# Stick-breaking attention and short convolution layer on one Trainium2 core: the last sixteen keys padded to 128 rows, Silu in one step, a first phase in written order, and a square root in the last norm

## The chip, the cores and the metric

The kernel runs on one core of one Trainium2 chip. The time is device microseconds of one execution of the whole layer, from a matrix of 256 tokens by 4096 channels to one of the same shape. The kernel before took 1779.79 us (median of three runs, 1779.18 to 1781.87). A separate execution was profiled; its own time was 1778.96 us and its profile spans 1777.2 us. Engines have the profile's names: PE does matrix products (PEld is its loading of the stationary operand), DVE and POOL do elementwise work, ACT does activation functions, copies and casts, SP issues most of the transfers between HBM and on-chip memory.

## The reference

One layer: 16 learned meta tokens are put ahead of the 256 tokens (272 positions), normed, and projected by one 4096 x 16384 matrix into eight parts of 2048 columns. Four serve attention (q, k, v and a gate), four a short convolution (B, C, h and a gate z). Each half is multiplied by the Silu of its gate, normed in groups of 128 channels, and a 4096 x 4096 matrix maps both back.

```
h = rmsnorm(x, norm_g)
p = h @ w_in
q, k, v, g_attn, b_conv, c_conv, h_conv, z_conv = jnp.split(p, cuts, axis=-1)
o = stick_breaking_attention(heads(q), heads(k), heads(v))   # 16 heads of 128
o = group_rmsnorm(o * jax.nn.silu(g_attn), attn_norm_g, ATTN_HEADS)
y = b_conv * short_conv(c_conv * h_conv, conv_w)             # 3 taps
y = group_rmsnorm(y * jax.nn.silu(z_conv), conv_norm_g, CONV_GROUPS)
hs = x + jnp.concatenate([o, y], axis=-1) @ w_out
return rmsnorm(hs, final_norm_g)[:, N_META:]
```

Attention weights are `exp(log sigmoid(z_ts) + sum of log sigmoid(-z_tj) for s < j < t)` for keys s before query t. A query block of 128 tokens sees at most 272 keys: two full blocks of 128 and 16 more.

## The kernel before, in words

**Pieces.** The weights come as a written list of pieces of 128 x 1024 numbers (`in_pieces`, and the output matrix behind it). For every piece SP loads `raw`, ACT casts it into a high part `wh` (line 409), DVE subtracts to get the low part `wl` (line 405), and PE multiplies three times, low activations by `wh`, high by `wh`, high by `wl` (lines 442 to 444 and 450 to 453), so that products of rounded parts make up a float32 product. Casts run four pieces ahead of PE (`SPLITS`), loads seven; `wh` and `wl` each have six buffers (`RING`), so ACT can cast piece i only when PE is done with piece i - 6.

**Groups.** Eight groups hold two heads and two convolution channel groups each. Pieces "A" and "B" belong to the parts q, g, B and z, which all 272 positions or 256 tokens need in full; "p" pieces make the blocks k, v, c and h of one head. From group 1 on, A and B pieces are multiplied as seven products instead of eight, with sums of tokens kept or reread (`sum`, `lent`), and two more pieces "T" and "U" are sums of A and B made by DVE (lines 426 to 431). Groups 8 to 11 are the output matrix, and eight thin pieces "o" close the list.

**Order.** A loop over pieces (`for i in range(1 - SPLITS, n)`) issues loads, PE's products and casts, and then runs tasks whose place was set by `later(piece, function)`. `plan_group` places the attention of group g: gates (`silu`), transposes of q, `scores`, `weights`, `trans`, `po` (the product of weights with values), `squares`, `norm`, `mix`. For the last group these places are counted in pieces behind its own end, `after(f, k)`. From the piece after group 0's own A and B pieces on, instructions stand on their engines in written order (`manual_schedule`, entered at `i == top[0] + 1`); ahead of that, and for the last eight pieces, a scheduler orders them. All engines take their instructions in order.

**Places that the prediction uses.** `po_mm` (line 806): five products per head. Four contract 128 keys; the fifth, line 812, contracts the last 16, with `a3` (16 x 128, weights) and `v3` (16 x 128, values). `vcopies` (line 596): ACT copies the transposed values into `vv` (16 copies of 32 x 64, line 576 in `blocks`) and `v3` (4 copies, line 605). For head 15, the last, the transpose stands at slot 13U and the copies behind slot 14U of group 7, ahead of that group's end. `silu` (line 668): ACT computes a sigmoid into a buffer, POOL multiplies it into the gate. `prep_x`: for each pair of channel blocks of x, scale by the norm's gain, cast, subtract; `finish_stats`: the rms factors of all positions, at the end of group 0. `finish(t)` (line 986): the last norm of token half t; for t = 1 it is the end of the program. It makes the reciprocal square root by nine small DVE instructions (an integer start value and two polynomial steps), then scales the 4096 columns in five parts and stores each. `WARM` products of constants stand ahead of the first piece.

Of the kernel before, what the change touches and what calls it, by code (L numbers as in the profile page):

```python
# [15 lines left out]
P = 128  # L16
D = 4096
# [20 lines left out]
WARM = 10  # L38
# [82 lines left out]
def kernel(ctx, tc, xt, xin, xm, par, fg, w1, w2, out):  # L121
# [7 lines left out]
    wk.tile([P, 46], F32, name="pad_wk")  # L129
# [16 lines left out]
    nc.vector.memset(ones, 1.0 / P)  # L146
    warm = bank("warm")
# [79 lines left out]
    rt2 = const.tile([P, 2], F32, name="rt2")  # L227
# [38 lines left out]
    def prep_x(j, parts=1):  # L266
        t = xr.pop(j)
        x = xs[j // 2][:, 2 * (j % 2):2 * (j % 2) + 2, :, :L]
        for i in range(2):
            g = pt[:, G0 + 2 * j + i:G0 + 2 * j + i + 1]  # L270
            if i or parts == 2:
                nc.vector.tensor_scalar(out=t[:, i, :], in0=t[:, i, :], scalar1=g, scalar2=None, op0=ALU.mult)
            else:
                nc.scalar.mul(out=t[:, i, :], in_=t[:, i, :], mul=g)
            if parts == 2:
                nc.scalar.copy(out=x[:, i, 0, :], in_=t[:, i, :])
                nc.vector.tensor_tensor(out=x[:, i, 1, :], in0=t[:, i, :], in1=x[:, i, 0, :].bitcast(F32), op=ALU.subtract)
        if parts == 1:
# [41 lines left out]
    def token_sums(dst, t, j):  # L320
        f = raw_sums(t, j)
        nc.scalar.copy(out=dst[:, 0], in_=f)
        nc.vector.tensor_tensor(out=dst[:, 1], in0=f, in1=dst[:, 0].bitcast(F32), op=ALU.subtract)

    mixh, mixl = [], []
# [41 lines left out]
    def split(i):  # L367
        p = pieces[i]
        if p[:2] == ("A", 0):
            prep_x(p[2], 2 if p[2] == 0 else 1)  # L370
        parts = 2 if i < 2 else 1
# [35 lines left out]
        for q in range(parts):  # L407
            c = slice(q * w // parts, (q + 1) * w // parts)
            nc.scalar.copy(out=h[:, c], in_=t[:, c])  # L409
            if parts == 2:  # L410
                low(c)
        if parts == 2:
# [33 lines left out]
    def mm_p(key, j, a, h, lo):  # L446
# [3 lines left out]
        nc.tensor.matmul(out=o, lhsT=a[1], rhs=h, start=key not in begun, stop=False)  # L450
        begun.add(key)
        nc.tensor.matmul(out=o, lhsT=a[0], rhs=h, start=False, stop=False)  # L452
        nc.tensor.matmul(out=o, lhsT=a[0], rhs=lo, start=False, stop=last)  # L453
        left[key] -= 1
# [31 lines left out]
    def mm_in(i):  # L486
# [4 lines left out]
        if p[0] == "p":  # L491
# [6 lines left out]
            return  # L498
        for q, st, c in works(i)[p[0]]:
# [3 lines left out]
            mm_p(key, p[2], st, wh[:, c], wl[:, c])  # L503
# [42 lines left out]
    def finish_stats():  # L546
# [18 lines left out]
        V.tensor_tensor(out=rt2, in0=rt, in1=rt, op=ALU.mult)  # L565
        for q in range(4):
            V.tensor_scalar(out=fac[:, 2 * q:2 * q + 2], in0=rt if q < 2 else rt2, scalar1=RS, scalar2=None,
                            op0=ALU.mult)
# [17 lines left out]
    def v_block(u, src, at_, at2):  # L586
# [4 lines left out]
        def vtrans():  # L591
            y = wk.tile([P, 416], F32, tag="zs", name=f"yv{u}")
# [3 lines left out]
        def vcopies(y):  # L596
            vv = wk.tile([P, 2 * P], F32, tag=f"vv{u % 2}", name=f"vv{u}")
            for i, k in enumerate((0, 1, 1, 1) if u < 2 else (0, 0, "p", 1) if u % 2 else (0, 0, "p", "p")):
# [3 lines left out]
            yield 1 if u < 2 else 0 if u % 2 else "p"  # L602
            v3 = wk.tile([META, P], F32, tag=f"v3{u % 2}", name=f"v3{u}")
            for i in range(4):
                A.copy(out=v3[:, 32 * i:32 * i + 32], in_=y[32 * i:32 * i + META, 2 * P:2 * P + 32])
# [24 lines left out]
    def plain_block(u, b, e):  # L630
# [17 lines left out]
    def evict(g):  # L648
# [4 lines left out]
        if g:  # L653
            p1, p5, p7, p6 = (psum.pop((g, q)) for q in (P1, P5, P7, P6))
            A.copy(out=cq[:, 0], in_=p1)
            for o, x, y, op in ((cb[:, 0], p6, cq[:, 0], ALU.add), (cq[:, 1], p7, cb[:, 0], ALU.add),
                                (cq[:, 0], d11, cq[:, 0], ALU.add), (cb[:, 1], p5, cq[:, 1], ALU.subtract),
# [10 lines left out]
    def silu(g, q):  # L668

        z = gr[g][q][1]  # L670
        s = wk.tile([P, 2, 2, P], F32, tag="u2", name=f"sg{q}{g}", bufs=2)
        for t in range(2):
            A.activation(out=s[:, t], in_=z[:, t], func=AF.Sigmoid, scale=rt[:, t:t + 1])
# [488 lines left out]
```

## Time and profile before

| | |
|---|---|
| median of three runs | 1779.79 us (1779.18 to 1781.87) |
| the profiled execution's own time | 1778.96 us |
| its span in the profile | 1777.2 us |
| around the span | 1.8 us |
| busy PE / PEld | 1762.1 / 1601.6 us |
| busy DVE / ACT / POOL | 1590.3 / 1233.1 / 151.0 us |
| moved by DMA | 410.96 MB, 231 GB/s |
| granted clock of PE over the span | 0.998 |

A timeline row reads: start, duration, engine, line, operation, written tile <- read tiles, shape, count, and in brackets how long the engine was idle ahead of it and what ended that. Products are pipelined on PE: the duration of a row is longer than the step to the next one, so rates are read from the starts. One product of two float32 operands stands as two records (x2).

### The profile page before, as it was taken

Reading aid. Unit: us, or ns where it says so; the run is one execution under the profiler, and the core shown is the slowest. Engines: PE = TensorE matmul, PEld = TensorE weight load, DVE = VectorE, ACT = ScalarE, POOL = GpSimd, SP = SyncE. Lnnn points to the kernel's source line nnn. Section 1 sums busy time; section 2 is a strip of 40 time slices with the busy share of each in tenths; the row PEclk is TensorE's granted clock in tenths of the full one; section 3 lists DMA queues with packets and bytes.
Section 4 is the critical chain, followed back from the end, with each engine's and each line's share of the span. In section 5 each row is a group of like instructions: output and inputs, shape, how many; then the busy total and the mean of one; then the engine's idle time right before and its main releaser. Section 6 shows DMA issues by size and latency. Waiting matters only on the chain.

```text
span 1777.2 us, 29833 instructions
## 1 busy us (share of the span) xinstructions
PE 1762.1 (99%) x10926; PEld 1601.6 (90%) x10926; DVE 1590.3 (89%) x1929; ACT 1233.1 (69%) x2089; POOL 151.0 (8%) x184
## 2 busy tenths in 40 slices
PE   9999999999999999999999999999999999999997
PEld 7899999999999999999999999999999988888897
DVE  6776898999999999999999999999999888989986
ACT  6755677677767776777678768776777785555553
POOL 2143110011001100010101010101010110000000
PEclk9999999999999999999999999999999999999999
DMA  8977666766676667666766676667666676676565
GB/s 316 323 238 249 226 214 216 259 214 226 218 251 219 225 226 245 215 230 222 250 215 228 213 257 215 225 218 245 213 231 226 228 236 233 231 233 213 196 224 191
DMA packets 120819, 410.96 MB, mean 231 GB/s; under 512 B 13536, under 2 KB 18784, under 8 KB 120672
## 3 DMA queue, kind: packets, MB, share of 16 engines
q1 hardware_dynamic: 116640, 405.38, 67.3%
q10 hardware_dynamic: 4032, 3.67, 0.6%
q8 instruction: 86, 1.41, 0.3%
q14 instruction: 61, 0.50, 0.1%
HBM read 395.37 MB, written 13.63 MB: 230 GB/s over the span
## 4 chain that ended last, share of the span: by engine, by line
PE 97%; DMA 1%; ACT 1%; DVE 0%; SPq 0%; issue 0%; POOL 0%; DVEq 0%; ACTq 0%
PE P L450 17%; PE P L453 17%; PE P L452 17%; PE mm L444 14%; PE mm L443 14%; PE mm L442 14%; PE mo L955 0%; PE mo L954 0%; PE mo L953 0%; PE z L755 0%; PE po L812 0%; DMA mixd<-mfh 0%; ACT wh L409 0%; DMA raw<-w 0%; PE z L754 0%; DVE wl L405 0%
## 5 line engine op out<-in xcount | busy, mean ns | idle before, releaser
L405 DVE TENSOR_TENSOR wl<-raw,wh 128x1024 fp32r<-128x1024 f32 (+3 forms) x780 | 862.2, 1135 | 77.9 <-ACT wh L409 72.2
L409 ACT CAST wh<-raw 128x1024 fp32r<-128x1024 f32 (+3 forms) x780 | 721.0, 965 | 278.0 <-PE mm L443 68.2
L442 PE MATMUL mm<-xs,wh 128*128 128x258 f32 (+1 forms) x2048 | 582.5, 284 | 0.4 <-ACT wh L409 0.4
L444 PE MATMUL mm<-xs,wl 128*128 128x258 f32 (+1 forms) x2048 | 581.7, 284 | 0.8 <-DVE wl L405 0.8
L443 PE MATMUL mm<-xs,wh 128*128 128x258 f32 (+1 forms) x2048 | 581.7, 284 | 0.0
L442 PEld LDWEIGHTS mm<-xs,wh 128*128 128x128 f32 x2048 | 385.5, 188 | 4.6 <-ACT wh L409 0.8
L443 PEld LDWEIGHTS mm<-xs,wh 128*128 128x128 f32 x2048 | 385.7, 188 | 3.7
L444 PEld LDWEIGHTS mm<-xs,wl 128*128 128x128 f32 x2048 | 385.7, 188 | 1.0 <-DVE wl L405 1.0
L409 ACT CAST wh<-t 128x1024 fp32r<-128x1024 f32 (+1 forms) x132 | 137.7, 1043 | 142.9 <-DVE t L426 123.9
L450 PE MATMUL P<-wh,xs 128*128 128x512 f32 x464 | 180.8, 390 | 1.2 <-ACT wh L409 1.2
L453 PE MATMUL P<-wl,xs 128*128 128x512 f32 x464 | 180.7, 390 | 0.2 <-DVE wl L405 0.2
L452 PE MATMUL P<-wh,xs 128*128 128x512 f32 x464 | 180.5, 389 | 0.0
L405 DVE TENSOR_TENSOR wl<-t,wh 128x1024 fp32r<-128x1024 f32 (+1 forms) x132 | 158.7, 1202 | 8.8 <-ACT wh L409 8.8
L426 DVE TENSOR_TENSOR t<-raw,raw 128x1024 f32<-128x1024 f32 (+1 forms) x132 | 164.9, 1250 | 0.0
L450 PE MATMUL P<-wh,mixl 128*128 128x512 f32 (+1 forms) x412 | 155.7, 378 | 0.0
L453 PE MATMUL P<-wl,mixh 128*128 128x512 f32 (+1 forms) x412 | 155.1, 376 | 0.0
L452 PE MATMUL P<-wh,mixh 128*128 128x512 f32 (+1 forms) x412 | 155.0, 376 | 0.0
L450 PE MATMUL P<-wh,lent 128*128 128x512 f32 x308 | 123.6, 401 | 0.0
L453 PE MATMUL P<-wl,lent 128*128 128x512 f32 x308 | 120.2, 390 | 0.0
L452 PE MATMUL P<-wh,lent 128*128 128x512 f32 x308 | 120.1, 390 | 0.0
L450 PEld LDWEIGHTS P<-wh,xs 128*128 128x128 f32 x464 | 87.1, 188 | 19.8 <-ACT wh L409 1.4
L453 PEld LDWEIGHTS P<-wl,xs 128*128 128x128 f32 x464 | 87.1, 188 | 19.3 <-DVE wl L405 1.1
(238 smaller groups left out, 2136.5 us busy)
## 6 DMA issues: line engine op xcount, KB each, us to landing
raw<-w SPq DMA_DIRECT2D x614, 512.0 KB, 4.5
lent<-sumd SPq DMA_DIRECT2D x77, 512.0 KB, 5.9
raw<-w SPq DMA_DIRECT2D x32, 384.0 KB, 3.8
sumd<-lent SPq DMA_DIRECT2D x11, 512.0 KB, 5.2
raw<-xin SPq DMA_DIRECT2D x8, 512.0 KB, 5.4
raw<-mixd SPq DMA_DIRECT2D x8, 512.0 KB, 4.6
xr<-xt SPq DMA_DIRECT2D x15, 272.0 KB, 4.9
res<-xin SPq DMA_DIRECT2D x12, 256.0 KB, 4.9
```

The lines of the kernel that those rows point to most:

```text
L405: nc.vector.tensor_tensor(out=lo[:, c], in0=t[:, c], in1=h[:, c].bitcast(F32), op=ALU.subtract)
L409: nc.scalar.copy(out=h[:, c], in_=t[:, c])
L426: nc.vector.tensor_tensor(out=s[:, :2 * hw].rearrange("p (a b) -> p a b", a=2), in0=a[:, :2 * hw].rearrange("p (a b) -> p a b", a=2), in1= ...
L442: nc.tensor.matmul(out=o, lhsT=h, rhs=x[:, 0, s:], start=k == 0, stop=False)
L443: nc.tensor.matmul(out=o, lhsT=h, rhs=x[:, 1, s:], start=False, stop=False)
L444: nc.tensor.matmul(out=o, lhsT=lo, rhs=x[:, 0, s:], start=False, stop=k == KC - 1)
L450: nc.tensor.matmul(out=o, lhsT=a[1], rhs=h, start=key not in begun, stop=False)
L452: nc.tensor.matmul(out=o, lhsT=a[0], rhs=h, start=False, stop=False)
L453: nc.tensor.matmul(out=o, lhsT=a[0], rhs=lo, start=False, stop=last)
```

## The change

1. **Padding.** `a3` and the two `v3` tiles have 128 rows instead of 16. They are zeroed once at the start, and only their first 16 rows are ever written. The product at line 812 contracts 128 rows.
2. **Silu.** ACT computes Silu into the gate itself; the sigmoid buffer and POOL's product are gone. The gate now holds the factor `rt` already, so `squares` and `fac` lose one `rt`.
3. **Written order from the first instruction.** `manual_schedule` is entered at the first turn of the loop. The first five pieces (`PARTS`) instead of two are cast in halves; the first two multiply both column halves by `wh` ahead of `wl`; the first pair of x is prepared half by half between the casts; a copy of one column (`first`) stands at the head of ACT; pairs 1 and 2 are scaled on ACT alone; sums kept for later are cast behind the B piece; `WARM` is 9.
4. **Last group.** Head 15's transpose and copies move from slots 13U and 14U to two and three pieces behind the group's end, into a `u2` buffer, one piece apart; `po`, the second `trans`, `squares` of the heads, `norm` and `mix` stand one piece later. Two of the sums in `evict` change places.
5. **Last norm.** ACT computes the square root, DVE its reciprocal and one correcting step.

```diff
-WARM = 10
+WARM = 9
+PARTS = 5
-    wk.tile([P, 46], F32, name="pad_wk")
+    wk.tile([P, 70], F32, name="pad_wk")
+    first = wk.tile([P, P], F32, tag="junk", name="first")[:, :1]
+    nc.scalar.copy(out=first, in_=ones[:, :1])
-    a3 = const.tile([META, P], F32, name="a3")
+    a3 = const.tile([P, P], F32, name="a3")
     nc.vector.memset(a3, 0.0)
+    v3s = [const.tile([P, P], F32, name=f"v3{u}") for u in range(2)]
+    for u in range(2):
+        nc.gpsimd.memset(v3s[u], 0.0)
...
         for q in range(parts):
             c = slice(q * w // parts, (q + 1) * w // parts)
+            if i == 0:
+                prep_x(0, q)
             nc.scalar.copy(out=h[:, c], in_=t[:, c])
+            if i == 0 and q == 0:
+                nc.vector.tensor_scalar(out=xr[0][:, 1, :], in0=xr[0][:, 1, :], scalar1=pt[:, G0 + 1:G0 + 2], scalar2=None, op0=ALU.mult)
             if parts == 2:
                 low(c)
+        while held and p[0] == "B":
+            held.pop()()
...
-            yield 1 if u < 2 else 0 if u % 2 else "p"
-            v3 = wk.tile([META, P], F32, tag=f"v3{u % 2}", name=f"v3{u}")
+            yield 1 if u in (0, 1, 15) else 0 if u % 2 else "p"
+            v3 = v3s[u % 2]
             for i in range(4):
-                A.copy(out=v3[:, 32 * i:32 * i + 32], in_=y[32 * i:32 * i + META, 2 * P:2 * P + 32])
+                A.copy(out=v3[:META, 32 * i:32 * i + 32], in_=y[32 * i:32 * i + META, 2 * P:2 * P + 32])
...
-                                    ((slot(g, 14, "p"), slot(g + 1, 1, "U")) if u < 15 else (slot(g, 13, "U"), slot(g, 14, "U"))) if u % 2 else
+                                    ((slot(g, 14, "p"), slot(g + 1, 1, "U")) if u < 15 else (after(fin[g], 2), after(fin[g], 3))) if u % 2 else
...
         for t in range(2):
-            A.activation(out=s[:, t], in_=z[:, t], func=AF.Sigmoid, scale=rt[:, t:t + 1])
-            G.tensor_tensor(out=z[:, t], in0=z[:, t], in1=s[:, t], op=ALU.mult)
+            A.activation(out=z[:, t], in_=z[:, t], func=AF.Silu, scale=rt[:, t:t + 1])
...
-        later(after(f, 13), po, g, 0)
-        later(after(f, 13), trans, g, 1)
-        later(after(f, 17), po, g, 1)
+        later(after(f, 14), po, g, 0)
+        later(after(f, 14), trans, g, 1)
+        later(after(f, 18), po, g, 1)
...
+        nc.scalar.activation(out=s, in_=sqs[t], func=AF.Sqrt, scale=1.0 / D, bias=acc[t])
         v.scalar_tensor_tensor(out=x, in0=sqs[t], scalar=1.0 / D, in1=acc[t], op0=ALU.mult, op1=ALU.add)
-        v.tensor_scalar(out=y.bitcast(I32), in0=x.bitcast(I32), scalar1=-0.5, scalar2=SEED,
-                        op0=ALU.mult, op1=ALU.add)
...
+        v.tensor_scalar(out=x, in0=x, scalar1=-0.5, scalar2=None, op0=ALU.mult)
+        v.reciprocal(out=y, in_=s)
         v.tensor_scalar(out=u, in0=y, scalar1=y, scalar2=x, op0=ALU.mult, op1=ALU.mult)
...
+        v.tensor_scalar(out=u, in0=u, scalar1=1.5, scalar2=y, op0=ALU.add, op1=ALU.mult)
...
-        if i == top[0] + 1:
+        if i == 1 - SPLITS:
             fixed = ExitStack()
             fixed.enter_context(tc.manual_schedule())
```

Where instructions stand now is shown at three places. First, the head of ACT's queue, before; `xs` is the cast x, `wh` the cast weights, line 409 one cast.

```order
L276 ACT_TABLE_LOAD
L276 CAST xs_134<-xr_151 128x272 x2
L409 CAST wh_176<-raw_153 128x512 x2
L409 CAST wh_182<-raw_157 128x512 x2
L274 ACTIVATE xr_160<-xr_160,pt 128x272
```

The same place in the changed kernel, where line 283 is the cast of x and line 424 that of weights:

```order
L149 ACT_TABLE_LOAD
L149 COPY first<-ones 128x1
L283 CAST xs_138<-xr_155 128x272
L424 CAST wh_176<-raw_157 128x512
L283 CAST xs_138<-xr_155 128x272
L424 CAST wh_176<-raw_157 128x512
L424 CAST wh_188<-raw_161 128x512 x2
L281 ACTIVATE xr_164<-xr_164,pt 128x272 x2
```

The table load no longer stands with the first cast that waits for x, and the first weights are cast behind one half of x instead of both.

Second, ACT at the end of group 7, before; `yv` holds head 15's transposed values, lines 576 and 605 are the copies, line 655 opens `evict`.

```order
L409 CAST wh_15654<-raw_15611 128x512
L576 COPY vv_15658<-yv_15608 32x2x32 x8
L409 CAST wh_15698<-t_15657 128x1024
L576 COPY vv_15658<-yv_15608 32x2x32 x4
L409 CAST wh_15732<-raw_15611 128x1024
L576 COPY vv_15658<-yv_15608 32x2x32 x4
L605 COPY v_15739<-yv_15608 16x32 x4
L409 CAST wh_15753<-raw_15646 128x1024
```

The copies in the changed kernel, behind line 775, the copy of q's transpose (line 746 before); lines 794 and 796 belong to the scores:

```order
L775 COPY cq_15758<-qT_15861 128x4x128
L606 COPY vv_15899<-yv_15868 32x2x32 x4
L424 CAST wh_15931<-raw_15799 128x1024
L606 COPY vv_15899<-yv_15868 32x2x32 x4
L424 CAST wh_15947<-raw_15832 128x1024
L424 CAST wh_15998<-raw_15871 128x1024
L794 ACTIVATE zl_0_16002<-zm_0_16001 128x416
L794 ACTIVATE zl_1_16007<-zm_1_16006 128x416
L796 ACTIVATE zl_0_16002<-zl_0_16002 128x416
L796 ACTIVATE zl_1_16007<-zl_1_16007 128x416
L606 COPY vv_15899<-yv_15868 32x2x32 x4
```

The twenty copies have left the seven-product pieces and stand in groups of four between the casts for the output matrix.

Third, DVE at the end of the program, before: from the last sum of squares to the first scaled columns.

```order
L989 SCALAR_TENSOR_TENSOR fin_0_19196<-sq_16038,acc_16036 128x1
L990 TENSOR_SCALAR fin_2_19198<-fin_0_19196 128x1
L992 TENSOR_SCALAR fin_1_19197<-fin_0_19196 128x1
L993 TENSOR_SCALAR fin_4_19200<-fin_2_19198,fin_0_19196 128x1
L994 TENSOR_SCALAR fin_2_19198<-fin_4_19200,fin_2_19198 128x1
L995 TENSOR_SCALAR fin_4_19200<-fin_2_19198,fin_1_19197 128x1
L996 TENSOR_SCALAR fin_3_19199<-fin_2_19198 128x1
L997 TENSOR_SCALAR fin_4_19200<-fin_4_19200 128x1
L998 TENSOR_SCALAR fin_4_19200<-fin_4_19200,fin_3_19199 128x1
L1003 TENSOR_SCALAR res_16034<-res_16034,fin_4_19200 128x256
```

And now, where `fin_1` is the square root that ACT writes:

```order
L1019 SCALAR_TENSOR_TENSOR fin_0_19136<-sq_15970,acc_15968 128x1
L1020 TENSOR_SCALAR fin_0_19136<-fin_0_19136 128x1
L1021 RECIPROCAL fin_2_19138<-fin_1_19137 128x1
L1022 TENSOR_SCALAR fin_3_19139<-fin_2_19138,fin_0_19136 128x1
L1023 TENSOR_SCALAR fin_3_19139<-fin_3_19139,fin_2_19138 128x1
L1028 TENSOR_SCALAR res_15966<-res_15966,fin_3_19139 128x256
```

Nine small instructions have become five, and the third of them waits for ACT. ACT's table of functions is loaded once more than before, ahead of the square root of token half 0; every other load stands where it stood.

More of the change, by code (lines that the diff above doesn't have):

```diff
@@ L264, in load_x, with prep_x @@
         xr[j] = t
-    def prep_x(j, parts=1):
-        t = xr.pop(j)
+    def prep_x(j, c=None):
+        t = xr.pop(j) if c is None else xr[j]
         x = xs[j // 2][:, 2 * (j % 2):2 * (j % 2) + 2, :, :L]
-        for i in range(2):
+        for i in range(2) if c is None else (c,):
             g = pt[:, G0 + 2 * j + i:G0 + 2 * j + i + 1]
-            if i or parts == 2:
+            if c == 1:
+                pass
+            elif i and j > 2 or c == 0:
                 nc.vector.tensor_scalar(out=t[:, i, :], in0=t[:, i, :], scalar1=g, scalar2=None, op0=ALU.mult)
@@ L321, in token_sums, with rest @@
         f = raw_sums(t, j)
-        nc.scalar.copy(out=dst[:, 0], in_=f)
-        nc.vector.tensor_tensor(out=dst[:, 1], in0=f, in1=dst[:, 0].bitcast(F32), op=ALU.subtract)
+        def rest():
+            y = f
+            nc.scalar.copy(out=dst[:, 0], in_=y)
+            nc.vector.tensor_tensor(out=dst[:, 1], in0=y, in1=dst[:, 0].bitcast(F32), op=ALU.subtract)
+        held.append(rest)
+    held = []
     mixh, mixl = [], []
@@ L368, in split @@
         p = pieces[i]
-        if p[:2] == ("A", 0):
-            prep_x(p[2], 2 if p[2] == 0 else 1)
-        parts = 2 if i < 2 else 1
+        if p[:2] == ("A", 0) and i:
+            prep_x(p[2])
+        parts = 2 if i < PARTS else 1
         if p[0] == "x":
@@ L444, in mm_k, with mm_p @@
         nc.tensor.matmul(out=o, lhsT=lo, rhs=x[:, 0, s:], start=False, stop=k == KC - 1)
-    def mm_p(key, j, a, h, lo):
+    def mm_p(key, a, h, lo):
         o = psum[key][:, :hwid(key[0])]
         last = left[key] == 1
[L450 to L454, printed above, removed]
+        if h is not None:
+            for q in (0, 1) if lo is None else (1, 0):
+                nc.tensor.matmul(out=o, lhsT=a[q], rhs=h, start=key not in begun, stop=False)
+                begun.add(key)
+        if lo is not None:
+            nc.tensor.matmul(out=o, lhsT=a[0], rhs=lo, start=False, stop=last)
+            left[key] -= 1
     begun, left = set(), {}
@@ L498, in mm_in @@
             return
+        lows_ = []
         for q, st, c in works(i)[p[0]]:
@@ L502, in mm_in @@
                 psum[key] = bank(f"P{q}_{p[1]}", (q + 4 * p[1]) % 8)
-            mm_p(key, p[2], st, wh[:, c], wl[:, c])
+            if i < 2:
+                mm_p(key, st, wh[:, c], None)
+                lows_.append((key, st, None, wl[:, c]))
+                if len(lows_) < 2:
+                    continue
+                for t in lows_:
+                    mm_p(*t)
+                lows_.clear()
+            else:
+                mm_p(key, st, wh[:, c], wl[:, c])
     def block_bank(i):
@@ L564, in finish_stats @@
         V.tensor_scalar(out=rq, in0=rt, scalar1=1.0 / math.sqrt(P), scalar2=None, op0=ALU.mult)
[L565 to L568, printed above, removed]
+        V.memset(fac[:, :4], RS)
+        for q in range(2, 4):
+            V.tensor_scalar(out=fac[:, 2 * q:2 * q + 2], in0=rt, scalar1=RS, scalar2=None, op0=ALU.mult)
     def blocks(dst, src, n, i, engines):
@@ L803, in trans @@
         A.copy(out=at[:META, P - META:P], in_=y[96:96 + META, 400:416])
-        A.copy(out=a3[:, P - META:], in_=y[96:96 + META, 432:448])
+        A.copy(out=a3[:META, P - META:], in_=y[96:96 + META, 432:448])
     def po_mm(g, u, o):
@@ L881, in plan_group @@
         later(after(e, 7), conv_out, g)
-        later(after(f, 13), po, g, 0)
-        later(after(f, 13), trans, g, 1)
-        later(after(f, 17), po, g, 1)
+        later(after(f, 14), po, g, 0)
+        later(after(f, 14), trans, g, 1)
+        later(after(f, 18), po, g, 1)
         later(after(f, 17), squares, g, "c")
-        later(after(f, 19), squares, g, "h")
-        later(after(f, 20), norm, g)
-        later(after(f, 22), mix, g, "h")
-        later(after(f, 23), mix, g, "c")
+        later(after(f, 20), squares, g, "h")
+        later(after(f, 21), norm, g)
+        later(after(f, 23), mix, g, "h")
+        later(after(f, 24), mix, g, "c")
     res, fgs, acc, sqs = [], {}, [], []
```

25 lines of the change are left out of this document (9 added, 16 removed).

## The prediction

> **What bounds the kernel now.** I read the page's busy shares first.
>
> ```profile
> PE 1762.1 (99%) x10926; PEld 1601.6 (90%) x10926; DVE 1590.3 (89%) x1929; ACT 1233.1 (69%) x2089; POOL 151.0 (8%) x184
> ```
>
> PE is busy for 1762.1 of 1777.2 us, so a change pays only if it shortens what PE itself does, removes one of PE's waits, or shortens the time ahead of its first product or behind its last. The view of PE's waits says how little there is of the second (waited-for tile and line, us in total, times, longest):
>
> ```profile
> PE P L450 <- ACT wh L409: 1.2, 1, 1.2
> PE mm L444 <- DVE wl L405: 0.8, 1, 0.8
> PE mm L442 <- ACT wh L409: 0.4, 1, 0.4
> ```
>
> The first is the start, the other two belong together and come at 1401 us. Which engine is next to bind is seen by stretches; columns are span and sum, then busy time of PE, PEld, DVE, ACT and POOL, granted clock, DMA share, GB/s:
>
> ```profile
> 748.00:792.00 44.00, 44.00 (x290) 40.32 (x289) 43.13 (x47) 34.83 (x67) 7.29 (x9) 1.00 0.66 221
> 792.00:836.00 44.00, 44.00 (x274) 39.76 (x273) 38.64 (x51) 32.91 (x67) 0.11 (x1) 1.00 0.63 205
> ```
>
> Inside a group DVE is within 0.87 us of full in one quarter, and has 5.36 us to spare in the next; ACT has 9 us everywhere.
>
> **The change part by part.** *Padding.* PE's timeline at one head's weights times values (starts are what count; a row x2 is one float32 product):
>
> ```profile
> 257.18 0.39 PE L810 MATMUL po<-vv,at 128*128 128x128 f32 x2
> 257.40 0.39 PE L811 MATMUL po<-vv,at 128*128 128x128 f32 x2
> 257.72 0.48 PE L812 MATMUL po<-v,a 16*128 16x128 f32 x2
> 258.13 0.50 PE L450 MATMUL P<-wh,lent 128*128 128x512 f32 x1
> 258.47 0.39 PE L452 MATMUL P<-wh,lent 128*128 128x512 f32 x1
> ```
>
> Products with 128 rows follow each other every 0.22. The one with 16 rows starts 0.32 behind L811, what follows starts 0.41 behind it, and even the next product takes 0.34. From L811 to L452 it is 1.07 us. What the same stretch takes with 128 rows throughout is shown by the transposes of the mix, four small products with 128 rows, then the same wide ones:
>
> ```profile
> 328.28 0.60 PE L716 MATMUL mxh<-ident,cq 128*128 128x128 f32 x4
> 328.64 0.48 PE L450 MATMUL P<-wh,lent 128*128 128x512 f32 x1
> 328.96 0.39 PE L452 MATMUL P<-wh,lent 128*128 128x512 f32 x1
> ```
>
> From their start to L452 it is 0.68; less four small ones at 0.11 (half of 0.22) that leaves 0.24 for the wide product behind them. A padded head thus takes 0.22 for L811, 0.22 for L812 and 0.24 for the return, 0.68, against 1.07: 0.39 saved, and with 16 heads 6.2 us. Were the return as slow as now (0.34), it would be 0.29 and 4.6. Nothing is added: the zeros are written once, on POOL, which is 8% busy. Casts must follow PE 6.2 us faster over the whole span; that needs DVE to gain 0.9 us in each of the seven groups, and the stretch with 5.36 us to spare gives it. I take −6.2.
>
> *Start.* The timeline of the first 19 us, with the landing of the first half of weights (issue at 1.7, landing 3.2 later) from the view of its line:
>
> ```profile
> L358 SPq DMA_DIRECT2D raw<-w x1: 423/423/423, 1.7 to 1.7; - x1
> ...
> DMA to landing us min/median/max: 3.2/3.2/3.2
> ```
>
> ```profile
> 1.12 4.52 PE L149 MATMUL warm<-ones 128*128 128x128 f32 x20 [1.12 <-DVE ones L146]
> ...
> 3.90 1.28 ACT L276 ACT_TABLE_LOAD   x1 [3.90 <-DMA xr<-xt]
> 3.94 0.36 DVE L272 TENSOR_SCALAR xr<-xr,pt 128x272 f32<-128x272 f32 x1 [2.15 <-DMA xr<-xt]
> ...
> 6.20 1.66 ACT L409 CAST wh<-raw 128x512 fp32r<-128x512 f32 x3
> ...
> 9.38 0.52 ACT L274 ACTIVATE xr<-xr,pt 128x272 f32<-128x272 f32 x1 [0.24 <-DMA raw<-w]
> ...
> 10.22 0.65 ACT L279 CAST xs<-xr 128x544 fp32r<-128x544 f32 x1 [0.32 <-DVE xr L272]
> ...
> 10.90 0.73 DVE L280 TENSOR_TENSOR xs<-xr,xs 128x544 fp32r<-128x544 f32 x1 [0.77 <-ACT xs L279]
> ```
>
> ```profile
> 6.87 0.50 PE L450 MATMUL P<-wh,xs 128*128 128x512 f32 x1 [1.23 <-ACT wh L409]
> ...
> 12.46 0.39 PE L450 MATMUL P<-wh,xs 128*128 128x512 f32 x1
> ...
> 18.03 0.39 PE L450 MATMUL P<-wh,xs 128*128 128x512 f32 x1
> ...
> 18.71 0.39 PE L450 MATMUL P<-wh,xs 128*128 128x512 f32 x1
> ```
>
> Before, ACT loads its table only once x has come (3.90 to 5.18), casts x twice, and casts weights from 6.20; PE's first real product is at 6.87. With the copy ahead, the load is done while x is on its way. ACT can cast half of x when DVE's scaling ends, 3.94 + 0.36 = 4.30, and is done near 4.8; weights have landed at 1.7 + 3.2 = 4.9; one cast, a third of 1.66, brings PE to about 5.6 with a step between engines: 1.25 earlier.
>
> That gain meets a new limit. The first two pieces are 24 products; at 0.227 each (18.03 to 18.71 is three) they last 5.5 us, so PE is ready for the third near 11.2 rather than 12.46. The third needs the second pair of x: both halves are now scaled on ACT from about 9.4 (two at 0.52), then a cast of 0.65 and a subtraction of 0.73, so near 11.7. PE loses 0.5. But 24 products from 12.46 should end at 17.9 and end at 18.71, so before lost 0.8 in the next two pieces, where halves let `wl` come sooner; I give those pieces back half, 0.4. At the fifth piece 1.25 − 0.5 + 0.4 = 1.15, and I take −1.2. Bounds: −0.6 if x comes later still, −2.0 if none of the 1.25 or the 0.8 is lost.
>
> *Last group.* ACT's timeline, then PE's:
>
> ```profile
> 1393.68 2.03 ACT L576 COPY vv<-yv 32x64 f32<-32x64 f32 x8
> ...
> 1400.13 0.90 ACT L605 COPY v<-yv 16x32 f32<-16x32 f32 x4
> 1401.05 1.05 ACT L409 CAST wh<-raw 128x1024 fp32r<-128x1024 f32 x1
> ```
>
> ```profile
> 1401.36 0.39 PE L453 MATMUL P<-wl,lent 128*128 128x512 f32 x1
> 1402.15 0.39 PE L442 MATMUL mm<-xs,wh 128*128 128x258 f32 x1 [0.41 <-ACT wh L409]
> 1402.37 0.28 PE L443 MATMUL mm<-xs,wh 128*128 128x258 f32 x1
> 1403.41 0.39 PE L444 MATMUL mm<-xs,wl 128*128 128x258 f32 x1 [0.76 <-DVE wl L405]
> 1403.63 0.28 PE L442 MATMUL mm<-xs,wh 128*128 128x258 f32 x1
> ```
>
> Sixteen copies at 0.25 and four more (0.90) take 4.9 us of ACT between the casts; the cast at 1401.05 comes late, PE stands, then stands again for `wl`. The steps are 0.79 where 0.23 is the rule, 1.04 and twice 0.22 where 0.12 is the rule for the shorter products (half of the 0.23 of wide ones): 0.56 + 0.92 + 0.2 = 1.7 us. The change takes all twenty copies from ahead of this point. They now stand four at a time (1 us) between output-matrix casts, where ACT has none of the group's other work in a row; six buffered pieces cover 1 us. I take −1.7, bounds 0 and −1.7.
>
> *Last norm.* DVE's timeline at the end, and one small ACT operation (softmax sums of 16 columns) as its measure:
>
> ```profile
> 1766.83 0.16 DVE L989 SCALAR_TENSOR_TENSOR fin<-sq,acc 128x1 f32<-128x1 f32 x1
> ...
> 1767.21 0.27 DVE L993 TENSOR_SCALAR fin<-fin,fin 128x1 f32<-128x1 f32 x1
> ...
> 1767.77 0.27 DVE L995 TENSOR_SCALAR fin<-fin,fin 128x1 f32<-128x1 f32 x1
> ...
> 1768.58 1.81 DVE L1003 TENSOR_SCALAR res<-res,fin 128x256 f32<-128x256 f32 x3
> ```
>
> ```profile
> 1436.31 0.20 ACT L790 ACTIVATE za<-zs 128x16 f32<-128x16 f32 x1
> ```
>
> The chain takes 1.75 (1766.83 to 1768.58). Now the root takes ACT 0.2 to 0.3 from 1766.83; the reciprocal starts near 1767.1 and takes 0.2; two dependent steps (0.56, the starts from 1767.21 to 1767.77) end it at 1767.87: −0.7, bounds −0.3 and −0.9. The added table load (1.28) stands in the other half's norm, whose stores aren't last.
>
> *At nothing:* Silu for sigmoid (same shape on ACT; POOL's product was off the path), the retained factor `rt`, the swapped sums, the zeros. `finish_stats` in written order can hold ACT up by 0 to 1 us under six buffered pieces' cover; 0.
>
> Sum: −6.2 − 1.2 − 1.7 − 0.7 = −9.8. The profiled execution (1778.96, of it 1.8 around the span) becomes 1769.2; it lies 0.83 under the median, so the median becomes **1770.0**.
>
> **The rivals.**
>
> *The padding gives nothing.* The 0.39 may belong to the change of accumulator or to small products as such. For it: the 16-row product is also the last of its five. Against it: the mix's small products return to wide ones in 0.24. Then 1770.0 + 6.2 = 1776.2, 7%. The Trainium skill (TensorE: Matmul & The Clock Gate, Part 2, step by step) states that streaming costs one cycle per column and that row count K doesn't matter; by that alone padding saves nothing, and the rows here, 0.32 and 0.41 against 0.22, disagree.
>
> *The moved copies make a new stall.* Head 15's `po` now waits for copies in the stretch from 1413 to 1450, and PE takes its products in order. If one group of copies or one cast is late there, the 1.7 comes back: 1771.7, and at 1 us a group for three groups at most 1774.9. 13%.
>
> *DVE becomes the bound* (the other side). With tiles of 128 rows placed anew and PE quicker, DVE would be on the path in the quarter where it has 43.13 of 44. It decides if DVE's subtractions grow by over 2% (0.87 of 43.13), and costs what the buffered pieces don't cover: at 8% and with no cover 43.13 becomes 46.6, PE waits 2.6 us in each of seven groups and never gets it back, +18, so 1770 + 18 = 1788. Nothing in the change lengthens a subtraction. 3%.
>
> *PE starts at half rate.* The constants at the start run at 4.52 / 20 = 0.226 a record, against 0.11 for the small products above. At 6.87 the rate is full. If full rate isn't there until 6.87, products from 5.6 on lose up to half of 1.27, 0.63: 1770.6 at most, as part of it is covered by the wait for x. 8%. The Trainium skill (same page, Part 1) lets full rate begin after one busy window of 3.4 us that doesn't start with the kernel, so by it as late as 7.9, an estimate that would cost 1.2.
>
> **How the numbers follow.** The sum as worked out has the rest, 69%. Its bounds: padding 4.6 to 6.2, start 0.6 to 2.0, copies 0 to 1.7, end 0.3 to 0.9. All low would be 1774.3, all high 1769.0; 0.7 below that for gains I don't see gives 1768.3, and the new stall's worst case takes the top to 1775.0. That leaves out the first and third rival and little more. A measurement of this kernel can tell about 0.2% from no change: under 1776.2 is faster, over 1783.4 slower. Faster has 93% (half of the first rival lies at the line), same 4%, slower 3%.
>
> **What would show it.** Padding right: L812's successor starts 0.22 behind its pair, and L450 to L452 is about 0.24, in every head. Start right: first real product near 5.6, fifth piece 1.2 earlier than 18.71. Copies: no PE wait between 1385 and 1450. End: the scaling starts 1.0 to 1.1 behind the sum of squares. I am wrong if PE shows waits for `wl` inside groups (DVE), or for `vv` or `v` behind the last group, or if the steps at L812 stay at 0.32 and 0.41.

## The result, and the profile after

The changed kernel takes **1769.88 us** (median of six runs, 1769.57 to 1770.70) against 1779.66 for the kernel before in the same comparison (six runs, 1777.83 to 1781.87). The ratio is 0.9945, with an interval from 0.9932 to 0.9958, so 7.5 to 12.1 us less. The forecast was 1770.0. The profiled execution spans 1768.1 us against 1777.2: its trace accounts for 9.1 us, not for 9.8, because the execution of the kernel before that was profiled (1778.96) was itself 0.7 us under its median.

The page's busy shares, and the view of PE's waits as far as it concerns real products:

```profile
PE 1755.2 (99%) x10924; PEld 1598.3 (90%) x10924; DVE 1574.8 (89%) x1920; ACT 1233.1 (70%) x2098; POOL 113.2 (6%) x154
```

```profile
PE P L471 <- ACT wh L424: 1.0, 1, 1.0
```

Only the wait at the start is left; the two at 1401 us are gone. The stretches inside a group:

```profile
748.00:792.00 44.00, 44.00 (x293) 40.49 (x292) 41.97 (x46) 34.56 (x67) 7.13 (x8) 1.00 0.67 228
792.00:836.00 44.00, 44.00 (x279) 40.15 (x278) 40.18 (x53) 32.59 (x68) 0.11 (x1) 1.00 0.65 214
```

PE is full in both. DVE seems to have 2.0 us to spare where it had 0.87, but the changed kernel is some 3.4 us further in its work at these times. The stretch with the same work shows 0.98 to spare:

```profile
744.50:788.50 44.00, 44.00 (x294) 40.54 (x293) 43.02 (x47) 34.78 (x67) 7.28 (x9) 1.00 0.64 220
```

PE is full there too, and waits for nothing behind its start: DVE did not become the bound.

*Padding.* PE's timeline at the same head as before (line 841 is the padded product, 471 and 474 the wide ones):

```profile
256.21 0.39 PE L840 MATMUL po<-vv,at 128*128 128x128 f32 x2
256.44 0.39 PE L841 MATMUL po<-v,a 128*128 128x128 f32 x2
256.58 0.71 PE L471 MATMUL P<-wh,lent 128*128 128x512 f32 x2
257.13 0.40 PE L474 MATMUL P<-wl,lent 128*128 128x512 f32 x1
```

The padded product starts 0.23 behind the fourth instead of 0.32. The wide one is 0.14 behind it instead of 0.41; its successor, inside the x2 row, then takes 0.31. The step of 0.03 between the padded product's second record and the wide one and this 0.31 together make the return. From the fourth product to the second wide one it is 0.68 by the records' starts, as forecast, against 1.07. The next few steps are some ns longer than before, so that a head keeps 0.37, and 16 heads 5.9 us.

*Start.* ACT and DVE, then PE, in the first 18 us:

```profile
0.80 1.28 ACT L149 ACT_TABLE_LOAD   x1 [0.80 <-PEq L1179]
...
4.05 0.36 DVE L279 TENSOR_SCALAR xr<-xr,pt 128x272 f32<-128x272 f32 x1 [2.24 <-DMA xr<-xt]
...
4.45 0.42 ACT L283 CAST xs<-xr 128x272 fp32r<-128x272 f32 x1 [2.17 <-DVE xr L279]
...
5.03 0.62 ACT L424 CAST wh<-raw 128x512 fp32r<-128x512 f32 x1 [0.17 <-DMA raw<-w]
```

```profile
5.70 1.21 PE L471 MATMUL P<-wh,xs 128*128 128x512 f32 x4 [0.97 <-ACT wh L424]
...
11.62 0.70 PE L471 MATMUL P<-wh,xs 128*128 128x512 f32 x2
12.39 0.50 PE L474 MATMUL P<-wl,xs 128*128 128x512 f32 x1
...
17.52 0.61 PE L471 MATMUL P<-wh,xs 128*128 128x512 f32 x2
```

The first real product is 1.17 earlier, the fifth piece (17.52 against 18.71) 1.19. The third piece begins at 11.62, and PE loses time there as forecast, though mostly for the low weights behind it (0.47 from the second of the two products at 11.62 to the one at 12.39, where 0.23 is the rule).

*Last group.* ACT, then PE at the place of the old stall:

```profile
1391.88 4.85 ACT L424 CAST wh<-raw 128x1024 fp32r<-128x1024 f32 x5 [1.00 <-DVE raw L450]
...
1408.21 1.01 ACT L606 COPY vv<-yv 32x64 f32<-32x64 f32 x4
1409.24 1.05 ACT L424 CAST wh<-raw 128x1024 fp32r<-128x1024 f32 x1
```

```profile
1395.25 0.39 PE L474 MATMUL P<-wl,lent 128*128 128x512 f32 x1
1395.48 0.28 PE L461 MATMUL mm<-xs,wh 128*128 128x258 f32 x1
1395.61 0.28 PE L462 MATMUL mm<-xs,wh 128*128 128x258 f32 x1
```

Five casts follow each other where copies stood between them, and PE goes over in steps of 0.23 and 0.13. The copies stand behind 1408 and PE waits for none of them.

*Last norm:*

```profile
1758.39 0.29 ACT L1018 ACTIVATE fin<-sq,acc 128x1 f32<-128x1 f32 x1
1758.39 0.16 DVE L1019 SCALAR_TENSOR_TENSOR fin<-sq,acc 128x1 f32<-128x1 f32 x1
...
1758.71 0.16 DVE L1021 RECIPROCAL fin<-fin 128x1 f32<-128x1 f32 x1
...
1759.47 1.81 DVE L1028 TENSOR_SCALAR res<-res,fin 128x256 f32<-128x256 f32 x3
```

1.08 from the sum of squares to the scaling, against 1.75.

### The profile page after: what moved, and what is told of

Same layout as the page of the kernel before. It is cut to its first block, busy times and chain, and to the rows that moved or that the text cites. A ratio compares the mean times of both kernels' runs of the same rounds, so it can differ in the third digit from the quotient of the medians.

```text
span 1768.1 us, 29789 instructions
## 1 busy us (share of the span) xinstructions
PE 1755.2 (99%) x10924; PEld 1598.3 (90%) x10924; DVE 1574.8 (89%) x1920; ACT 1233.1 (70%) x2098; POOL 113.2 (6%) x154
## 4 chain that ended last, share of the span: by engine, by line
PE 99%; DMA 0%; DVE 0%; SPq 0%; ACT 0%; issue 0%; DVEq 0%; ACTq 0%
PE P L471 35%; PE P L474 18%; PE mm L462 14%; PE mm L461 14%; PE mm L463 14%; PE mo L984 0%; PE mo L983 0%; PE mo L982 0%; PE z L784 0%; DMA xr<-xt 0%; PE z L783 0%; PE po L838 0%; PE po L841 0%; PE po L839 0%; PE po L840 0%; PE po L837 0%
## 5 line engine op out<-in xcount | busy, mean ns | idle before, releaser
L471 PE MATMUL P<-wh,xs 128*128 128x512 f32 x928 | 285.5, 390 | 1.0 <-ACT wh L424 1.0
L471 PEld LDWEIGHTS P<-wh,xs 128*128 128x128 f32 x928 | 174.1, 188 | 38.1 <-ACT wh L424 1.2
L471 PE MATMUL P<-wh,lent 128*128 128x512 f32 x616 | 193.5, 395 | 0.0
L445 DVE TENSOR_TENSOR t<-raw,raw 128x1024 f32<-128x1024 f32 (+1 forms) x132 | 160.9, 1219 | 0.0
L471 PEld LDWEIGHTS P<-wh,lent 128*128 128x128 f32 x616 | 109.5, 188 | 17.3
L450 DVE TENSOR_TENSOR raw<-raw 128x512 f32<-128x512 f32 (+1 forms) x132 | 91.5, 694 | 4.6
```

What stands on the lines that cost most here:

```text
L445: nc.vector.tensor_tensor(out=s[:, :2 * hw].rearrange("p (a b) -> p a b", a=2), in0=a[:, :2 * hw].rearrange("p (a b) -> p a b", a=2), in1= ...
L450: nc.vector.tensor_tensor(out=t[:, c1], in0=t[:, c1], in1=t[:, c2], op=ALU.add)
L471: nc.tensor.matmul(out=o, lhsT=a[q], rhs=h, start=key not in begun, stop=False)
```

## The experiments

The theory under test is the prediction's: four separate gains, most of it from 16 rows becoming 128. The rivals are that the time at the fifth product is not the rows' (then padding alone does nothing), that another engine or a new wait takes the gain back, and that PE's rate at the start decides what the start gives. Each run's time stands beside the kernel before on the same chip.

**One part alone: the padding.**

```diff
-    a3 = const.tile([META, P], F32, name="a3")
+    a3 = const.tile([P, P], F32, name="a3")
+    v3s = [const.tile([P, P], F32, name=f"v3{u}") for u in range(2)]
...
-            v3 = wk.tile([META, P], F32, tag=f"v3{u % 2}", name=f"v3{u}")
+            v3 = v3s[u % 2]
```

> The kernel before with the padding alone (weights tile and both value tiles of the last sixteen keys at 128 rows). Theory (a product over 16 rows among products over 128 costs PE two slow changes): the step behind the last 128-row product falls from 0.32 to 0.22 us and the one behind the 16-row product from 0.41 to 0.22, and the kernel gains 0.37 us in each of 16 heads, 5.9 us: about 1773.8. Rival (the time belongs to the fifth product of a head, whatever its rows): steps stay at 0.32 and 0.41, 1779.7. Rival (DVE can't feed PE faster): steps shorten but PE waits for the low weights inside the groups, between 1774 and 1780.

Measured: 1773.72 against 1778.68, ratio 0.9969 (0.9957 to 0.9980), 5.0 us less by the medians and 3.6 to 7.6 by the interval. The trace has the same steps as the whole change:

```profile
258.08 0.39 PE L814 MATMUL po<-vv,at 128*128 128x128 f32 x2
258.30 0.39 PE L815 MATMUL po<-v,a 128*128 128x128 f32 x2
258.44 0.48 PE L453 MATMUL P<-wh,lent 128*128 128x512 f32 x1
```

The saving is the padding's own. That the product comes fifth and last does not matter.

**How many rows are enough.** The changed kernel with another number of rows in each pair of heads.

```diff
+ROWS = (16, 16, 32, 32, 48, 48, 64, 64, 96, 96, 112, 112, 128, 128, 16, 16)
...
-    T.matmul(out=o[:, P:SEQ], lhsT=a3, rhs=v3, start=False, stop=True)
+    r = ROWS[2 * g + u]
+    for c in range(2 if g == 7 else 1):
+        T.matmul(out=o[:, P:SEQ], lhsT=a3[:r], rhs=v3[:r], start=False, stop=g < 7 or c == 1)
```

> The changed kernel with the fifth product over another number of rows in each pair of heads: 16, 32, 48, 64, 96, 112, 128 for heads 0 to 13, and for the last two heads 16 rows twice over (the last sixteen keys are counted twice there). From the start of the fourth product to that of the second wide one behind took 1.07 us with 16 rows and 0.68 to 0.70 with 128. Theory A (any product over fewer rows than the full 128 is a change of mode and back): 16 to 112 rows all take 1.07. Theory B (rows are taken in some coarser unit, so that 96 or 112 count as full): the large ones take 0.70, the small ones 1.07, with a jump between. Theory C (cost grows with the rows missing): a slope from 1.07 down to 0.70. Where 16 rows stand twice, theories A and B expect the second one 0.22 behind the first, so 1.29 in all; if the row count itself were slow the second costs 0.3 or more.

Measured, from the fourth product to the second wide one, the same in both heads of a pair to 0.003: 16 and 32 rows 1.07, 48 and 64 rows 1.07, 96 rows 0.68, 112 and 128 rows 0.68. PE's timeline with 64, with 96, and with 16 rows twice over (x4):

```profile
784.01 0.39 PE L841 MATMUL po<-vv,at 128*128 128x128 f32 x2
784.33 0.48 PE L844 MATMUL po<-v,a 64*128 64x128 f32 x2
784.74 0.50 PE L472 MATMUL P<-wh,lent 128*128 128x512 f32 x1
```

```profile
959.79 0.39 PE L841 MATMUL po<-vv,at 128*128 128x128 f32 x2
960.01 0.39 PE L844 MATMUL po<-v,a 96*128 96x128 f32 x2
960.15 0.71 PE L472 MATMUL P<-wh,lent 128*128 128x512 f32 x2
```

```profile
1446.26 0.39 PE L841 MATMUL po<-vv,at 128*128 128x128 f32 x2
1446.57 0.71 PE L844 MATMUL po<-v,a 16*128 16x128 f32 x4
```

Theory B holds: up to 64 rows cost the full price, 96 cost nothing. A second product over 16 rows takes 0.22 (records 0.11 apart), so few rows are not slow: the change to them and back is. The Trainium skill (TensorEngine Tiling (Array Packing), Tiling Modes) states under Key Properties that a change of tiling mode drains the engine, and lists under Available Configurations modes of 32, 64 and 128 rows. The jump between 64 and 96 agrees with that, and the price of both changes together, 0.39 us, is this trace's. The kernel took 1774.29 in a single run, 4.4 over the changed kernel: ten of the sixteen heads pay again, 10 x 0.37 = 3.7, the two products more take 2 x 0.22 = 0.4, and the rest is within what starts differ by.

**One part alone: the last group.**

```diff
-    (slot(g, 13, "U"), slot(g, 14, "U"))
+    (after(fin[g], 2), after(fin[g], 3))
...
-        later(after(f, 13), po, g, 0)
+        later(after(f, 14), po, g, 0)
```

> The kernel before with the last group's new places alone. Theory (twenty copies on ACT ahead of the group's end delayed the casts): PE's waits at 1401 us go, 1.5 us gained, about 1778.2, and no wait comes between 1405 and 1450. Rival (the moved copies delay casts or the product of weights with values behind the group): a wait of 1 us or more there, 1779 to 1781.

Measured: 1778.59 against 1778.68, ratio 0.9998 (0.9989 to 1.0007). The time can't tell 1.5 us from nothing. The trace can: its only wait of PE for real products is at the start,

```profile
PE P L450 <- ACT wh L409: 1.9, 1, 1.9
```

and product for product PE gains 1.61 us on the kernel before between 1361 and 1421 us, with 1.29 lost ahead of 97 us, in the start that this kernel did not change. There PE's granted clock falls to half for 3.4 us (the last three columns are granted clock, DMA share, GB/s):

```profile
8.40:11.80 3.40, 3.40 (x10) 2.63 (x9) 2.39 (x5) 2.46 (x4) 1.57 (x3) 0.50 1.01 396
```

**One part alone: the start.**

```diff
-WARM = 10
+WARM = 9
+PARTS = 5
...
-        if i == top[0] + 1:
+        if i == 1 - SPLITS:
```

> The kernel before with the new start alone (early table load, halves, written order from the first instruction). Theory: first real product at 5.7 rather than 6.87, 1.2 us kept to the end, about 1778.5. Rival (a product that is earlier at 6 us meets a wait for x or for low weights later in the first group): less than 0.6 us kept at 100 us, 1779.2 or above.

Measured: 1778.15 against 1778.68, ratio 0.9995 (0.9986 to 1.0004). In the profiled execution the first real product is at 6.08, but the second pair of x came late (PE waits 1.1 for it), and the fifth piece begins at 18.91, later than in the profile before. The rival's case, in this execution. Starts differ that much between executions; so I collected all of them further down.

**One part alone: the last norm's root.**

```diff
+        nc.scalar.activation(out=s, in_=sqs[t], func=AF.Sqrt, scale=1.0 / D, bias=acc[t])
...
+        v.reciprocal(out=y, in_=s)
```

> The kernel before with the last norm's square root on ACT alone. Theory: last sum of squares to first scaling 1.1 us rather than 1.75, 0.7 us gained, about 1779.0, which a measurement can hardly tell from nothing but the trace can. Rival (the added table load or the hand-over between ACT and DVE eats it): 1.7 us or more from sum of squares to scaling, 1779.7 or above.

Measured: 1799.67 against 1778.68, ratio 1.0115 (1.0102 to 1.0129): **21 us slower**, a loss that neither expectation accounts for. Nothing waits for the root: product for product, PE loses about 0.9 us per 60 us evenly up to 1361 us, where 20.3 us are gone, long before the first square root, and only 1.0 in the 400 us of the output matrix behind it. What differs from the first product on is where tiles stand. The new norm has two small tiles less. In the compiled program these take 32 bytes a partition each, and every tile allocated behind them stands 64 bytes lower: the first weight tile at byte 60992 instead of 61056.

**Silu undone.** The changed kernel with sigmoid on ACT and the product on POOL.

```diff
-            A.activation(out=z[:, t], in_=z[:, t], func=AF.Silu, scale=rt[:, t:t + 1])
+            A.activation(out=s[:, t], in_=z[:, t], func=AF.Sigmoid, scale=rt[:, t:t + 1])
+            G.tensor_tensor(out=z[:, t], in0=z[:, t], in1=s[:, t], op=ALU.mult)
```

> The changed kernel with sigmoid on ACT and the product on POOL again instead of Silu. Theory (off the path): PE waits for nothing new, the same time within 0.5 us, about 1769.9, POOL's busy time 40 us higher. Rival (POOL's traffic to the same memory slows DVE or the gate comes late): 1 us or more slower, with DVE's subtractions longer.

Measured: 1784.93 against 1779.15, ratio 1.0032 (1.0020 to 1.0045), 15 us above the changed kernel. Again it can't be the arithmetic, since the loss grows evenly (1.5 us at 18 us, 14.4 at 1361 us, against the changed kernel) and PE waits only at the start. This kernel needs one small tile more (`rt2`), and its weight tiles stand 32 bytes higher.

So a new theory: PE's pace depends on where its two operands stand. Four runs test it, two that put the weight tiles back and two that only move them. In the first, the unused tile ahead of the work tiles grows by the 64 bytes.

```diff
-    wk.tile([P, 46], F32, name="pad_wk")
+    wk.tile([P, 62], F32, name="pad_wk")
```

> The square root alone again, with one unused tile 64 bytes larger. Without that, the two small tiles that the new norm saves moved every weight tile down by 64 bytes, the run took 1799.7 us, and its trace shows no wait of PE, but wide products a few ns slower all through. Theory (PE is slower where its two operands stand at different offsets in a block of memory): with the weight tiles back at their old addresses 1778.0, the 0.7 us of the shorter chain alone. Rival (the table load or the square root itself slows the kernel): 1799 again.

Measured: 1778.97 against 1778.96, ratio 1.0000 (0.9992 to 1.0009): the 21 us are gone, with the root on ACT as before. The chain is short as forecast, 1.08:

```profile
1767.82 0.16 DVE L990 SCALAR_TENSOR_TENSOR fin<-sq,acc 128x1 f32<-128x1 f32 x1
...
1768.90 1.81 DVE L999 TENSOR_SCALAR res<-res,fin 128x256 f32<-128x256 f32 x3
```

0.67 us is too little for these times to show.

The same for sigmoid, the unused tile smaller by 32 bytes:

```diff
-    wk.tile([P, 70], F32, name="pad_wk")
+    wk.tile([P, 62], F32, name="pad_wk")
```

> Sigmoid and POOL's product again in the changed kernel, with one unused tile 32 bytes smaller, so that the weight tiles stand where they stand in the changed kernel (without that: 1784.9). Theory (addresses): the same time as the changed kernel within 0.5 us, 1769.9. Rival (POOL's products slow PE or DVE by using the same memory): 1784 again.

Measured: 1771.11 against 1778.96, ratio 0.9957 (0.9944 to 0.9969), against the whole change's 0.9945 (0.9932 to 0.9958). 14 of the 15 us are gone. The 1.2 left were not forecast. Product for product this execution loses 1.7 us on the changed kernel's, all of it ahead of 52 us, and then nothing for 1000 us. It is the start again, not the sigmoid. One part of the rival did happen: DVE is busy 1587.1 us here and 1574.8 in the changed kernel. Of the 126 instructions at line 446 that make `t`, the 14 that run beside POOL's take 1.62 us, the 112 with POOL idle 1.22; without the sigmoid 7 run beside POOL's. PE waits for none of it.

Then the changed kernel with nothing but its unused tile as it was before the change:

```diff
-    wk.tile([P, 70], F32, name="pad_wk")
+    wk.tile([P, 46], F32, name="pad_wk")
```

> The changed kernel with one line of its change undone, the size of an unused tile (70 back to 46 columns), which moves the weight tiles down by 96 bytes. Theory (addresses): wide products with x as the stationary operand take 233 ns rather than 227, 13 to 22 us slower, about 1787. Rival (only the other two shifts were bad): 1770.

Measured: 1792.07 against 1778.96, ratio 1.0073 (1.0058 to 1.0089), **22 us above the changed kernel**. The view of waits and a stretch show nothing to wait for, with PE full at a granted clock of 1.00:

```profile
PE P L471 <- ACT wh L424: 0.8, 1, 0.8
```

```profile
748.00:792.00 44.00, 44.00 (x286) 40.26 (x286) 41.85 (x45) 32.36 (x56) 7.22 (x9) 1.00 0.68 228
```

It is in the pace. Eighteen wide products with x as the stationary operand, at the same place in this kernel and in the changed one:

```profile
42.69 0.63 PE L471 MATMUL P<-wh,xs 128*128 128x512 f32 x2
...
46.90 0.63 PE L471 MATMUL P<-wh,xs 128*128 128x512 f32 x2
```

```profile
39.96 0.61 PE L471 MATMUL P<-wh,xs 128*128 128x512 f32 x2
...
44.04 0.61 PE L471 MATMUL P<-wh,xs 128*128 128x512 f32 x2
```

4.21 us against 4.08. The busy view can't show this, since PE counts as busy in both.

Last, tiles 128 bytes lower:

```diff
-    wk.tile([P, 70], F32, name="pad_wk")
+    wk.tile([P, 38], F32, name="pad_wk")
```

> The changed kernel with the unused tile at 38 columns: weight tiles 128 bytes lower, so both operands are again at the same offset in a block of 128 bytes but not in one of 256. Theory with 256: the few products of the kernel before whose operands differ by 128 took 234 ns, so x against weights takes 233 to 234, 8 us or more slower, 1778 to 1788. Theory with 128: 1770.

Measured: 1790.41 against 1778.96, ratio 1.0066 (1.0052 to 1.0079). 128 bytes are no better than 96: the theory with blocks of 128 falls, the one with 256 stands so far.

The steps by operand, worked out from the starts of all records ahead of which another of the same width stands, with the addresses of the compiled program:

| kernel | weight tiles moved by | wide products, x stationary: ns (count) | x moving, 272 columns: ns | time |
|---|---|---|---|---|
| before | 0 | 227.1 (1293) | 123.4 | 1779.66 |
| changed | 0 | 227.2 (1287) | 123.4 | 1769.88 |
| root alone | -64 bytes | 232.8 (1297) | 125.4 | 1799.67 |
| sigmoid back | +32 | 233.4 (1295) | 123.6 | 1784.93 |
| unused tile 46 | -96 | 232.6 (1298) | 125.8 | 1792.07 |
| unused tile 38 | -128 | 233.0 (1293) | 126.6 | 1790.41 |

The tiles of x have fixed places at the other end. The slices of x that are stationary begin 64 bytes into a tile, behind the 16 meta tokens; they stand at the same place in a block of 256 bytes as the weight tiles in the first two kernels, and in no other of the six. Three more groups of wide products agree that this distance decides. Those whose stationary operand is `mixh` stay at 226.9 to 227.6 in all six; these tiles move along with the weights, which fits the small loss in the output matrix. Four tiles of `osum` stay put like x: some 120 products with them go from 227 to between 231.6 and 233.9 when the weights move. Two more move along, 128 bytes apart from the weights, and their 48 products take 234.0 in the kernel before and after too.

The other products do not follow that rule. Those of 272 columns begin at the start of a tile of x: their operands are 192 bytes apart (modulo 256) in the first two kernels, and in root alone, where they stand at the same place, they take 125.4 rather than 123.4. Products with `lent` and `sum` (1169 of them) are 1 to 4 ns longer in moved kernels though they moved along. So that addresses alone cost this time is shown by the four runs; that a block of 256 bytes decides is shown for wide products with x, `mixh` and `osum` alone; what decides for the rest, and what inside the chip makes it so, is open. For the last kernel, 5.8 ns x 1293 is 7.5 us and 3.2 ns x 3013 products of 272 columns 9.7 us, most of its 20; `lent` and `sum` add 2.7, and products of 258 columns, 0.9 ns shorter there, give 2.7 back.

**The start, undone in one place.**

```diff
-    first = wk.tile([P, P], F32, tag="junk", name="first")[:, :1]
-    nc.scalar.copy(out=first, in_=ones[:, :1])
```

> The changed kernel without the one-column copy at the head of ACT, so that the table load stands ahead of the first cast that waits for x. Theory (the early load is what moves the first product): the first real product comes 1.28 us later, near 6.9, of which 0.4 is saved again since the third piece then waits for nothing: 0.8 us slower at 100 us. Rival (halves and order move it, and the load would be hidden): first product below 6.0, no change.

Measured: 1770.97, ratio 0.9952 (0.9937 to 0.9967). ACT and PE:

```profile
4.70 1.28 ACT L281 ACT_TABLE_LOAD   x1 [4.70 <-DMA xr<-xt]
...
6.99 2.07 PE L469 MATMUL P<-wh,xs 128*128 128x512 f32 x4 [1.66 <-ACT wh L422]
```

The first product is 1.29 later than in the changed kernel's profile, but x also landed 0.7 later here (DVE scales it from 4.73 rather than 4.05). In the five profiles that have the copy and x from 4.69 to 4.75, the first product is at 6.08 to 6.24. So the early load is worth 0.75 to 0.9 of the 1.29. At 100 us this execution is 2.0 behind rather than the 0.8 expected, since its products step by 0.43 until 10.1; the times can't tell their 1.1 us from none.

**Fewer products of constants.**

```diff
-WARM = 9
+WARM = 3
```

> The changed kernel with three instead of nine products of constants ahead of the first piece. In its own trace these products' steps fall from 0.213 to 0.111 us at 3.97 us, 2.9 us after they begin. Theory (PE doubles its rate only after about 3 us of nearly unbroken work): the three end near 2.5, and the real products start at half rate, 0.45 a step, for 2 to 4 us, so the first piece ends 1 to 2 us later. Rival (the rate rises at a time of its own, whatever PE does): full rate, 0.23 a step, from the first real product on.

Measured: 1770.76 in a single run.

```profile
5.98 2.07 PE L471 MATMUL P<-wh,xs 128*128 128x512 f32 x4 [3.22 <-ACT wh L424]
...
8.71 1.60 PE L471 MATMUL P<-wh,xs 128*128 128x512 f32 x4
10.15 0.62 PE L474 MATMUL P<-wl,xs 128*128 128x512 f32 x2
10.61 1.07 PE L471 MATMUL P<-wh,xs 128*128 128x512 f32 x4
```

Real products start at 5.98 at half rate (six in 2.73, or 0.45 each), and between 8.71 and 10.61 the rate comes to the 0.23 of the rule. That is the theory's case. But the run with sigmoid and kept addresses, with nine constants, does the same:

```profile
1.12 4.21 PE L152 MATMUL warm<-ones 128*128 128x128 f32 x18 [1.12 <-DVE ones L147]
6.11 2.07 PE L472 MATMUL P<-wh,xs 128*128 128x512 f32 x4 [0.78 <-ACT wh L425]
7.98 1.05 PE L475 MATMUL P<-wl,xs 128*128 128x512 f32 x2
...
19.24 0.62 PE L472 MATMUL P<-wh,xs 128*128 128x512 f32 x2
```

Four products take 1.87 from 6.11, where the changed kernel's profile shows 1.17 from 5.70. So this test is inconclusive: the number of constants is not what decided.

**All starts together.** The fifth piece begins, with the old start, at 18.71 (before), 19.38 (padding alone), 19.39 (root alone), 19.68 (root kept) and 19.99 (last group alone): mean 19.43. With the new one it begins at 17.52 (changed), 18.07 (rows), 18.44 (unused tile 38), 18.91 (start alone), 19.03 (sigmoid), 19.24 (sigmoid kept) and 19.49 (unused tile 46): mean 18.67. (The two kernels that change the new start itself are left out: 19.54 without the copy, 18.77 with three constants.) The gain is 0.8 on average, and single executions spread over 2 us. In the last three of the new start, and in two of the old (padding alone, root kept), the real products begin at half rate; in a third of the old (last group alone) they fall back to it. The Trainium skill (TensorE: Matmul & The Clock Gate, Part 1) has the rate decided by a window that runs freely, so that the same kernel meets it differently from one execution to the next. These starts agree.

## Why the prediction was right

**The bound.** PE stayed the bound, with no new wait in the trace, so each part paid what it took from PE.

**Padding, 6.2 forecast, 5.9 measured.** The row that I took the price from, small products of 128 rows ahead of wide ones, was the right one, 0.68 in both. How the 0.68 was divided was not: 0.22, 0.22 and 0.24 were forecast, 0.22, 0.14 and 0.31 came, so the steps that were to show it (0.22 and 0.24 behind the padded product) did not, and only their sum did. The 0.3 less is a few ns in each of the steps that follow. The first rival (it gives nothing) fell by the padding alone and by the jump between 64 and 96 rows.

**Start, 1.2 forecast, 1.19 in the profiled execution, 0.8 on average.** In the profiled execution each term came as worked out: 1.17 at the first product (1.25 forecast), 0.84 at the third piece (0.75), 1.19 at the fifth (1.15). But that is the luckiest of the seven, and the term is too large by 0.4 on average: it assumed x and PE's rate as in one profile. The fourth rival (half rate at the start) got 8%; in the seven profiles with the new start whose fifth piece is listed above it happened three times. Its price of at most 0.63 rests on full rate by 6.87, and was too low: here products step by 0.43 until 9.7, 10.5 and 10.5, which is 3.6 to 4.4 us behind the first real one, and the fifth piece of these three is 1.0 later than that of the other four on average. Why the constants ahead of it did not count there is open. It cost the change little only because the old start suffers from it too.

**Last group, 1.7 forecast, 1.5 measured.** Both waits went. One of the slow restarts that I counted (0.1) came back elsewhere: the first product of the last group's own small pieces now takes 0.22. The second rival (new stalls) did not occur in this trace nor in the part alone. (Its worst case is 1771.7 and three times 1, which is 1774.7 and not 1774.9.)

**Last norm, 0.7 forecast, 0.67 measured.** The added table load is hidden as said.

**Silu at nothing** is supported by the run with kept addresses, within the spread of the start. That POOL's product was off the path is right for PE's waits; that it cost DVE 12 us of busy time was not foreseen, and did no harm here.

5.9 + 0.8 + 1.5 + 0.7 is 8.9. The median moved by 9.8 with an interval from 7.5 to 12.1, so that 1770.0 met 1769.88 this closely is partly luck.

**What it passed over.** The third rival had tiles placed anew slowing DVE's subtractions, at 3% and 18 us. Its price was about right and its engine wrong: moved tiles slow PE. The prediction took the line on the unused tile at nothing without naming it. In truth this line puts the weight tiles back where they were, at byte 61056, after the dropped `rt2` (32 bytes) and the smaller norm (64) had moved them by 96; without it the changed kernel is 10 to 16 us slower than the kernel before (1792.07). So the forecast held because the change itself undid a cost that the forecast did not contain.

## What to carry to other kernels

A short contraction between full ones (16 to 64 rows here) cost 0.39 us for going and coming back; padded with zeros to 96 rows or more it cost nothing of that, and the zeros are free where the tiles can stay zero. Where PE is the bound and a change adds or drops even a tile of one column, compare operand addresses and the steps between PE's starts ahead of any verdict on the change itself: no view of waits or busy time shows that loss. Sub-microsecond gains at the start and end have to be read from traces, and from several of them.

## What was not expected of the hardware

Moving the weight tiles by 32, 64, 96 or 128 bytes against x costs 14 to 22 us of 1780, at a granted clock of 1.00 and with no new wait: wide products with x as the stationary operand go from 227 to 233 ns, and those of 272 columns from 123.4 to as much as 126.6. And PE's rate at the start is not set by the work ahead alone. With the same eighteen records of constants it doubled at 4.0 us in one execution (records 0.21 apart, then 0.11), and near 10 us in others (wide products 0.43 apart, then 0.23).
